# Middle-sized experts of a MoE kernel as half and quarter blocks, with a new order of the ranks

## The chip, the cores and the metric

The kernel runs on one core of a Trainium2 chip. A time is device microseconds of one execution. Three runs of the kernel before are given, and their median stands for it. Beside them there is one profiled execution, whose trace is read here.

## The reference

One decoder block on 512 tokens of width 1024, all float32: a mixer (Mamba-2 SSD branch, pooling branch, gates), then a mixture of 32 experts, four to a token, then a norm. The change touches the experts alone:

```python
logits = xt @ w_router + b_router
top_val, top_idx = lax.top_k(logits, 4);  gate = softmax(top_val)
def expert_block(xblk, e):                  # rows of tokens of one expert
    gu = xblk @ w_gu[e] + b_gu[e]           # 1024 -> 2048
    glu, lin = split(gu, 2);  glu = min(glu, 7);  lin = clip(lin, -7, 7)
    act = glu * sigmoid(1.702 * glu) * (lin + 1)
    return act @ w_down[e] + b_down[e]      # 1024 -> 1024
y = segment_sum(yb * row_gate, row_tok)
```

How many of the 512 tokens go to an expert differs from expert to expert and is known only at run time.

## The kernel before, in words

After the mixer and the router the kernel sorts the 32 experts by their number of tokens into ranks. A table `ROOM` gives each rank its room, in rows of tokens: rank 0 has 128, ranks 1 to 15 have 64, ranks 16 to 26 have 72 to 96 (eleven ranks), ranks 27 to 30 have 108 to 128, rank 31 has 192. What does not fit is done in a loop behind everything, which runs as often as there are overflowing blocks. Each rank is a **step** of the main loop, and `order_of_ranks` writes the sequence of steps out by hand. In it `s` is a rank with room for 64, `f` one of ranks 16 to 30, `None` rank 31. Before, it reads: rank 0, s s, five pairs f s, rank 31, s, five pairs f s, five f in a row, s s.

Every step needs the expert's whole weights, 12 MB: eight 1 MB pieces of `w_gu` (128 rows of the contraction by 2048) and four of `w_down` (two contraction chunks by 1024). SyncE's queue fetches them (L772) into a ring of eleven 1 MB buffers, in the order of use; a fetch waits until its buffer has been read.

Step `u` does `up(u)`, the products with `w_gu`, and then `down(u-1)`, the products with `w_down` of the step before; hooks between the pieces hold the small work: `prep(u+2)` (which tokens, and a gather of their rows by GpSimd), `turned(u+1)` (transposes of the gathered rows), `act_turn` (activation of step u and its transposes), `send` (scaling by the gate and a scatter-add into DRAM by GpSimd). PSUM has two pools of four banks, `mm` and `ss`.

A rank is computed in one of two forms:

- **whole** (room over 64): `esplit` splits each piece into a rounded part (ScalarE, L117) and a remainder (VectorE, L118), and each product is three TensorE matmuls of 128 columns by 512 in the rounded type (L1119, L1120, L1121): 96 in `up`, 48 in `down`.
- **half** (room up to 64): no split; the 1 MB piece is used as it is, in float32, with 64 tokens as the stationary operand (L1114). Two output chunks lie on the two halves of the 128 PSUM partitions (`rows_of`), so that two matmuls of 64 columns use the array side by side: 32 in `up`, 16 in `down`. The trace has two records for each of these float32 matmuls.

Bias products (L1108 whole, L1105 half) open each group of banks, so their rows in the trace mark where an `up` (bank `mm`) or a `down` (bank `ss`) begins.

Of the kernel before, what the change touches and what calls it, by code (L numbers as in the profile page):

```python
# [20 lines left out]
P = 128  # L21
# [38 lines left out]


def order_of_ranks():
    s, f = iter(range(FIXED, FIXED + SMALL)), iter(range(FIXED + SMALL, NE - 1))
    kinds = [s, s] + [f, s] * 5 + [None, s] + [f, s] * 5 + [f] * 5 + [s, s]
    return list(range(FIXED)) + [next(k) if k else NE - 1 for k in kinds]


# [1 line left out]
def hybrid_block(ctx: ExitStack, tc: tile.TileContext, cst, cols, rows, xt, xf, wad0, wada, bada,  # L69
# [902 lines left out]
    def overflow_table():  # L972
        cap = cs[:, C_CAP:C_CAP + NE]
        ex, dcap, deid = rk["tmp"][:, 0:NE], rk["tmp"][:, NE:2 * NE], rk["eid"]
        nbk, tmp = T_("nbk", NE), T_("tmpe", NE)
        tt(ex, rk["cnt"], cap, ALU.subtract)
        V.tensor_scalar(nbk, ex, 0.0, None, op0=ALU.is_gt)
        for lim in (128.0, 256.0, 384.0):
            V.tensor_scalar(tmp, ex, lim, None, op0=ALU.is_gt)
            tt(nbk, nbk, tmp, ALU.add)  # L980
        ce = T_("ce", NE)
        V.tensor_tensor_scan(ce, ones[:, 0:NE], nbk, 0.0, op0=ALU.mult, op1=ALU.add)
        V.memset(dcap, 0.0)
        tt(dcap[:, 0:NE - 1], cap[:, 1:NE], cap[:, 0:NE - 1], ALU.subtract)
        stt(dcap, nbk, -128.0, dcap, ALU.mult, ALU.add)
        tt(tmp[:, 0:NE - 1], deid[:, 1:NE], deid[:, 0:NE - 1], ALU.subtract)
        V.memset(tmp[:, NE - 1:NE], 0.0)
        ruf, euf, ubase, eui, novi = T_("ruf", OVER), T_("euf", OVER), T_("ubase", OVER), T_("eui", OVER, I32), T_("novi", 1, I32)
        V.tensor_copy(novi, ce[:, NE - 1:NE])
        for u in range(0, OVER, 16):  # L990
            us_ = slice(u, u + 16)
            lev, lwv = (T_(t, 512).rearrange("p (u e) -> p u e", u=16) for t in ("q16", "q15"))
            tt(lev, ce.unsqueeze(1).to_broadcast([P, 16, NE]), iota[:, us_].unsqueeze(2).to_broadcast([P, 16, NE]), ALU.is_le)
            V.tensor_reduce(ruf[:, us_], lev, axis=AX.X, op=ALU.add)
            tt(lwv, lev, dcap.unsqueeze(1).to_broadcast([P, 16, NE]), ALU.mult)
            V.tensor_reduce(ubase[:, us_], lwv, axis=AX.X, op=ALU.add)
            tt(lwv, lev, tmp.unsqueeze(1).to_broadcast([P, 16, NE]), ALU.mult)
            V.tensor_reduce(euf[:, us_], lwv, axis=AX.X, op=ALU.add)
        V.tensor_scalar(ruf, ruf, float(NE - 1), None, op0=ALU.min)
        stt(ubase, iota[:, 0:OVER], 128.0, ubase, ALU.mult, ALU.add)  # L1000
        V.tensor_scalar(ubase, ubase, float(room(0)), None, op0=ALU.add)
        V.tensor_copy(eui, euf)
        return ruf, euf, ubase, eui, novi
# [4 lines left out]

    turned_rot = Rot(["q11"])

    class Op:
        def __init__(self, t, half):
            self.t, self.half = t, half
            if half:
                self.c = [t[:, k % 4 * P + k // 4 * 64:k % 4 * P + k // 4 * 64 + 64] for k in range(KD)]
            else:
                self.h, self.l = ([t[:, r * 1024 + k * P:r * 1024 + (k + 1) * P] for k in range(KD)] for r in range(2))

# [4 lines left out]

    def slots(i, pos, n_, xe):
        half = n_ <= 64
        s4 = T_(("a2", "wrt")[i % 2 if i != "x" else 0], 4 * P, BF16)
        for b in range(NB):
            o = s4[:, b * P:(b + 1) * P]  # L1030
            if half:
                V.tensor_scalar(o.rearrange("p (h m) -> p h m", h=2), iota1[:, 0:64].unsqueeze(1).to_broadcast([P, 2, 64]),
                                pos(b), None, op0=ALU.is_equal)
            else:
                V.tensor_scalar(o, iota1, pos(b), None, op0=ALU.is_equal)
        ps = bank("ss")
        for b in range(NB):
            sb_ = s4[:, b * P:(b + 1) * P]
            TE.matmul(ps[:, 0:2], sb_, tokc[:, 0:2], start=b == 0, stop=False)
            TE.matmul(ps[:, 0:2], sb_, tokc[:, 2 + 2 * b:4 + 2 * b], start=False, stop=b == NB - 1)  # L1040
        n = i if i == "x" else i % 6
        st = dict(s4=s4, ps=ps, xe=xe, n=n, half=half, rows=P if half else min(n_, P))
        ix_ = T_(f"ixs_{n}", 2)
        stt(ix_[:, 0:1], ps[:, 1:2], cs[:, C_NP:C_NP + 1], cs[:, C_P5:C_P5 + 1], ALU.mult, ALU.add)
        tt(ix_[:, 0:1], ps[:, 0:1], ix_[:, 0:1], ALU.add)
        if half:
            stt(ix_[:, 1:2], ix_[:, 0:1], 2.0, cs[:, C_H:C_H + 1], ALU.mult, ALU.add)
        idx = T_(f"idx_{n}", 1, I32)
        V.tensor_copy(idx, ix_[:, 1:2] if half else ix_[:, 0:1])
        src, lim, xe = (h_d2, 2 * T - 1, xe[:, 0:512]) if half else (h_d, T - 1, xe)  # L1050
        if i != 0:
            n_ = st["rows"]
            G.indirect_dma_start(xe[0:n_, :], None, src, bass.IndirectOffsetOnAxis(ap=idx[0:n_, :], axis=0), bounds_check=lim, oob_is_err=False)
        st.update(idx=idx, ixf=ix_[:, 0:1])
        return st
# [35 lines left out]
        return ps[n // 2][n % 2 * 64:n % 2 * 64 + 64, :]  # L1091

    lastp = []

# [2 lines left out]
            bias_rows(x, ps, sel, n0)  # L1099

    def bias_rows(x, ps, sel, n0):
        for n, p in enumerate(ps):
            if x.half:
                c = n0 // 2 + n
                TE.matmul(p, sel["wide"], bt[:, c * 512:(c + 1) * 512], start=True, stop=False)  # L1105
            else:
                h, c = (n0 + n) % 2, (n0 + n) // 2
                TE.matmul(p, sel["cols"][:, h:h + 1].to_broadcast([P, P]), bt[:, c * 512:(c + 1) * 512], start=True, stop=False)  # L1108

    def products(x, ps, k, hl, o, n0=0):  # L1110
        stop = k == KD - 1
        if x.half:
            for i in range(2):
                lastp[:] = [TE.matmul(rows_of(ps, n0 + i), x.c[k], hl[:, o + i * 512:o + (i + 1) * 512], start=False, stop=stop).ins]  # L1114
            return
        hi, lo = hl
        for i in range(2):
            p, h, l = ps[n0 + i], hi[i], lo[i]
            TE.matmul(p, x.h[k], h, start=False, stop=False)  # L1119
            TE.matmul(p, x.h[k], l, start=False, stop=False)  # L1120
            lastp[:] = [TE.matmul(p, x.l[k], h, start=False, stop=stop).ins]  # L1121
# [3 lines left out]
            yield o, esplit(r[:, o:o + 1024]) if full else None  # L1125

    def up(xs, sel, w, hooks):
        pss = [[bank("ss" if i else "mm") for _ in range(2 if x.half else 4)] for i, x in enumerate(xs)]
        for x, ps in zip(xs, pss):
            biases(x, ps, sel, 0)  # L1130
        for k in range(KD):
            r = eload(w, "wu", k)
            for o, hl in ahead.pop(0) if ahead else pieces(r, not xs[0].half):
                for x, ps in zip(xs, pss):
                    products(x, ps, k, r if x.half else hl, o, o // 512)
            for f in hooks.get(k, ()):
                f()
        return pss
# [14 lines left out]
    def act_rows(pg, pl_):  # L1153
# [5 lines left out]
        stt(l, l, 1.0, t, ALU.add, ALU.mult)  # L1159
        return l  # L1160

    def act_turn(l, aT, n):
        pt = turn_tile(l)
        if aT.half:
# [10 lines left out]
    def send(ps, st, tag="y"):  # L1175
        half, y = st["half"], T_(tag, 512 if st["half"] else 1024)
        for n, p in enumerate(ps):
            yn = y[:, n * 512:(n + 1) * 512]
            S.activation(yn, p, AF.Copy, scale=st["gate"])  # L1179
            G.tensor_tensor(yn, yn, gaf2[0] if half else gaf[n], op=ALU.mult)  # L1180
        dst, lim = (y_d2, 2 * (T + P) - 1) if half else (y_d, T + P - 1)
# [94 lines left out]
    def select(u):  # L1276
# [5 lines left out]
        for h in range(2 if both else 0):  # L1282
            hs = slice(h * 64, (h + 1) * 64)
            G.tensor_copy(wides[u % 2][hs, hs], e[hs, :].to_broadcast([64, 64]))

    def prep(u):
        if u < NE:
            sts[u] = slots(u, pos_of(u), room(order[u]), xe2[u % 2])
            if u > FIXED:
                slot_gates(sts[u], gv_of(u))  # L1290

    def turned(u):
        if u < NE:
            xs_[u] = [turn(sts[u], Rot(["y"]) if u == 1 else x_rot)]


# [62 lines left out]
    for u in range(NE + 1):  # L1359
        hooks = {}  # L1360
        if u < NE:
            w, sel = weights_of(u), sel_of(u)
            pre = {k: list(f) for k, f in extra.get(u, {}).items()}
            if u != 0:
                pre.setdefault(0, []).append(lambda: prep(u + 2))
            if u == big - 2:
                pre.setdefault(4, []).append(prep_x)
            if pend:
# [3 lines left out]
                pre[n] = [f] + pre.get(n, [])  # L1372
            begin = []
            pss = up(xs_[u], sel, w, pre)
            aTs = [op_of(Rot(["q16"]) if u == 1 else a_rot, xs_[u][0].half)]
            hooks = {n: [f] for n, f in enumerate(acts(pss[0], aTs[0]))}
            if u == big:
                aTs.append(op_of(Rot(["b12"]), True))
                lx = act_rows(*pss[1])
# [12 lines left out]
        else:  # L1392
# [6 lines left out]
            else:  # L1399
                send(psd[0], sts[v])  # L1400
                if len(psd) > 1:
                    pend.append(lambda p=psd[1]: send(p, sts["x"], "q16"))
        if u < NE:
            prev = (u, aTs)

# [136 lines left out]
```

## Time and profile before

| | |
|---|---|
| runs | 1824.81, 1825.79, 1829.6 us; median 1825.79 us |
| profiled execution | 1824.71 us, of which the span of instructions is 1822.9 us |
| TensorE busy in the span | 1739.8 us (95%) |
| VectorE, ScalarE, GpSimd busy | 1211.0, 947.8, 238.7 us |
| HBM traffic | 527.81 MB, 290 GB/s over the span |
| granted TensorE clock, mean | 0.995 of full speed |
| experts | from the first bias product at 696.87 us to the end |

The 1.8 us between span and time lie around the span. A busy TensorE in this profile is one that has a matmul in flight, which is not yet one that works at its peak.

### The profile page before, as it was taken

The numbers are of one execution on the slowest core, as the hardware profiler recorded it, in microseconds if no ns is written. First come the engines' busy times: TensorE is split into PE (matmuls) and PEld (weight loads), VectorE is DVE, ScalarE is ACT, GpSimd is POOL, SyncE is SP. The second block draws the span as 40 slices with busy tenths as digits, with TensorE's granted clock in tenths as the row PEclk, the third lists the DMA queues.
The fourth block names the chain that finished last, engine by engine and source line by source line (L and its number), as shares of the span: only waits on it lengthen the run. The fifth ranks groups of instructions, "written<-read, shape, count | busy, mean of one in ns | idle before, by whom it ended". The sixth has DMA issues, their size and how long they took to land. (4 is left out here: it accounts for less than half of the span.)

```text
span 1822.9 us, 23331 instructions
## 1 busy us (share of the span) xinstructions
PE 1739.8 (95%) x8353; PEld 1160.5 (64%) x8353; DVE 1211.0 (66%) x1803; ACT 947.8 (52%) x1458; POOL 238.7 (13%) x215
## 2 busy tenths in 40 slices
PE   6999999999999999999999999999999999999995
PEld 3787787877778777456556455464565565677741
DVE  5888686857574548666567556375585586799933
ACT  4533455637372346356455455265465465677833
POOL 0000001010100002121121211122112112222111
PEclk9999999999999999999999999999999999999998
DMA  9265333353553457999999999889999999998894
GB/s 358 75 243 220 116 119 135 116 118 114 127 151 135 170 220 296 360 410 401 408 407 403 400 392 335 307 324 378 399 404 396 402 405 364 412 348 340 311 375 189
DMA packets 86344, 527.81 MB, mean 290 GB/s; under 512 B 11737, under 2 KB 12377, under 8 KB 27600
## 3 DMA queue, kind: packets, MB, share of 16 engines
q1 hardware_dynamic: 74160, 498.14, 69.9%
q0 software_dynamic: 11184, 25.50, 6.6%
q10 hardware_dynamic: 880, 2.64, 0.4%
q8 instruction: 67, 1.10, 0.2%
q14 instruction: 53, 0.43, 0.1%
HBM read 502.89 MB, written 25.77 MB: 290 GB/s over the span
## 5 line engine op out<-in xcount | busy, mean ns | idle before, releaser
L118 DVE TENSOR_TENSOR wl<-r,wh 128x1024 fp32r<-128x1024 f32 x246 | 301.8, 1251 | 106.4 <-ACT wh L117 105.4
L117 ACT ACTIVATE wh<-r 128x1024 fp32r<-128x1024 f32 x246 | 254.6, 1058 | 125.1 <-PE mm L266 48.4
L118 DVE TENSOR_TENSOR wl<-S,wh 128x1024 fp32r<-128x1024 f32 x186 | 229.3, 1268 | 32.9 <-ACT wh L117 32.4
L1120 PE MATMUL mm<-wl,S 128*128 128x512 f32 x540 | 214.2, 397 | 8.1 <-DVE wl L118 7.9
L117 ACT ACTIVATE wh<-S 128x1024 fp32r<-128x1024 f32 x186 | 190.2, 1057 | 54.2 <-PE mm L1121 30.2
L1121 PE MATMUL mm<-wh,S 128*128 128x512 f32 x540 | 212.9, 394 | 0.0
L265 PE MATMUL mm<-S,wh 128*128 128x512 f32 x512 | 204.9, 401 | 3.9 <-ACT S L117 3.9
L267 PE MATMUL mm<-S,wl 128*128 128x512 f32 x512 | 203.8, 398 | 1.5 <-DVE wl L118 1.5
L266 PE MATMUL mm<-S,wh 128*128 128x512 f32 x512 | 204.1, 399 | 0.0
L1119 PE MATMUL mm<-wh,S 128*128 128x512 f32 x540 | 182.1, 400 | 1.9 <-ACT wh L117 1.4
L1155 DVE TENSOR_SCALAR q<-mm 128x512 f32<-128x512 f32 x49 | 33.5, 688 | 151.7 <-PE mm L1114 124.4
L1156 ACT ACTIVATE q<-q 128x512 f32<-128x512 f32 x50 | 31.6, 634 | 191.7 <-DVE q L1155 191.6
L1119 PEld LDWEIGHTS mm<-wh,S 128*128 128x128 f32 x540 | 101.1, 188 | 39.4 <-issue 9.7
L1120 PEld LDWEIGHTS mm<-wl,S 128*128 128x128 f32 x540 | 101.3, 188 | 37.2 <-DVE wl L118 14.2
L265 PEld LDWEIGHTS mm<-S,wh 128*128 128x128 f32 x512 | 96.3, 188 | 30.6 <-ACT S L117 4.1
L1121 PEld LDWEIGHTS mm<-wh,S 128*128 128x128 f32 x540 | 101.4, 188 | 21.8
L266 PEld LDWEIGHTS mm<-S,wh 128*128 128x128 f32 x512 | 96.3, 188 | 26.2 <-issue 4.6
L267 PEld LDWEIGHTS mm<-S,wl 128*128 128x128 f32 x512 | 96.3, 188 | 25.9 <-issue 2.2
L1120 PE MATMUL ss<-wl,S 128*128 128x512 f32 x240 | 98.8, 412 | 3.1 <-DVE wl L118 3.1
L1121 PE MATMUL ss<-wh,S 128*128 128x512 f32 x240 | 94.8, 395 | 0.0
L1114 PE MATMUL mm<-S,S 128*64 128x512 f32 x408 | 94.6, 595 | 0.0
L1180 POOL TENSOR_TENSOR y<-y,q 128x512 f32<-128x512 f32 x47 | 63.5, 1363 | 209.0 <-ACT y L1179 208.9
(500 smaller groups left out, 3072.8 us busy)
## 6 DMA issues: line engine op xcount, KB each, us to landing
S<-in_wgu SPq DMA_DIRECT2D x113, 1024.0 KB, 10.9
r<-in_wgu SPq DMA_DIRECT2D x97, 1024.0 KB, 9.9
S<-in_wdn SPq DMA_DIRECT2D x61, 1024.0 KB, 12.3
r<-in_wdn SPq DMA_DIRECT2D x44, 1024.0 KB, 13.9
bc<-in_wgu SPq DMA_DIRECT2D x23, 1024.0 KB, 11.5
Z<-in_wgu SPq DMA_DIRECT2D x23, 1024.0 KB, 9.5
r<-in_wada SPq DMA_DIRECT2D x16, 1024.0 KB, 6.0
r<-in_wx SPq DMA_DIRECT2D x12, 1024.0 KB, 6.4
```

Source lines behind the costliest of these rows:

```text
L117: S.activation(hi, src, AF.Copy)
L118: V.tensor_tensor(lo, src, hi.bitcast(F32), op=ALU.subtract)
L265: TE.matmul(ps, a, hh(k), start=k == 0, stop=False)
L266: TE.matmul(ps, a, hl(k), start=False, stop=False)
L267: TE.matmul(ps, b, hh(k), start=False, stop=k == KD - 1)
L1114: lastp[:] = [TE.matmul(rows_of(ps, n0 + i), x.c[k], hl[:, o + i * 512:o + (i + 1) * 512], start=False, stop=stop).ins]
L1119: TE.matmul(p, x.h[k], h, start=False, stop=False)
L1120: TE.matmul(p, x.h[k], l, start=False, stop=False)
L1121: lastp[:] = [TE.matmul(p, x.l[k], h, start=False, stop=stop).ins]
L1155: V.tensor_scalar(g, pg, LIM, None, op0=ALU.min)
L1156: S.activation(t, g, AF.Tanh, scale=ALPHA / 2)
L1180: G.tensor_tensor(yn, yn, gaf2[0] if half else gaf[n], op=ALU.mult)
```

## The change

The eleven ranks with room for 72 to 96 get a third form, **half and quarter**: the first 64 tokens go as a half block, the other 8 to 32 as a quarter block, in which the stationary operand is 32 columns wide and four output chunks lie on the four quarters of the PSUM partitions (`rows32`), so that four matmuls of 32 columns may stand side by side. Nothing is split for such a rank. It has its own slots, gather, transposes, activation (`act_quarter`), gate scaling and scatter (under the tag `q16`, one step later). In `down` the quarter block takes two contraction chunks at once, two quarters each, and `send` adds the two partial sums. The order is now: rank 0, s s, twice (w s f f f s), s, rank 31, s s, w s f f f, s w s f f s s s, where `f` is one of the eleven and `w` one of the four larger ranks, which stay whole. The table of overflow borrows another buffer.

```diff
 def order_of_ranks():
-    s, f = iter(range(FIXED, FIXED + SMALL)), iter(range(FIXED + SMALL, NE - 1))
-    kinds = [s, s] + [f, s] * 5 + [None, s] + [f, s] * 5 + [f] * 5 + [s, s]
+    s, f, w = (iter(r) for r in (range(FIXED, FIXED + SMALL), range(FIXED + SMALL, NE - 5), range(NE - 5, NE - 1)))
+    kinds = [s, s] + ([w, s] + [f] * 3 + [s]) * 2 + [s, None, s, s] + [w, s] + [f] * 3 + [s, w, s, f, f, s, s, s]
...
     def slots(i, pos, n_, xe, quarter=0):
...
+        if quarter:
+            G.memset(s4.rearrange("p (h m) -> p h m", m=64)[:, :, quarter:64], 0.0)
...
+    def rows32(ps, n):
+        o = n % 2 * 64 + n // 2 * 32
+        return ps[0][o:o + 32, :]
...
     def bias_rows(x, ps, sel, n0):
+        if x.quarter:
+            for n in range(4 if x.quarter == "up" else 2):
+                c, h = (n0 + n) // 2, n % 2
+                TE.matmul(rows32(ps, n), sel["wide"][:, h * 64:h * 64 + 32].bitcast(F32), bt[:, c * 512:(c + 1) * 512].bitcast(F32),
+                          start=True, stop=False)
+            return
...
     def products(x, ps, k, hl, o, n0=0):
         stop = k == KD - 1
+        if x.quarter == "up":
+            for n in range(4 if n0 else 0):
+                lastp[:] = [TE.matmul(rows32(ps, n), x.c[k], hl[:, n * 512:(n + 1) * 512], start=False, stop=stop).ins]
+            return
+        if x.quarter:
+            for n in range(4 if k % 2 else 0):
+                kk = k - 1 + n // 2
+                lastp[:] = [TE.matmul(rows32(ps, n), x.c[kk], hl[:, n * 512:(n + 1) * 512], start=kk == 1, stop=kk >= KD - 2).ins]
+            return
...
+    def act_quarter(p):
+        g, t, l = g_rot(), t_rot(), l_rot()
+        V.tensor_scalar(g, p, LIM, None, op0=ALU.min)
+        S.activation(t, g, AF.Tanh, scale=ALPHA / 2)
+        V.tensor_scalar(l, p, LIM, -LIM, op0=ALU.min, op1=ALU.max)
+        for o in (0, 64):
+            V.tensor_scalar(l[o:o + 32, :], p[o + 32:o + 64, :], LIM, -LIM, op0=ALU.min, op1=ALU.max)
+        stt(t, t, 1.0, g, ALU.add, ALU.mult)
+        stt(l, l, 1.0, t, ALU.add, ALU.mult)
+        return l
...
     def send(ps, st, tag="y"):
...
+            if st["quarter"]:
+                S.activation(yn, p, AF.Copy)
+                for o in (0, 64):
+                    S.activation(yn[o:o + 32, :], p[o + 32:o + 64, :], AF.Copy)
+                tt(yn, yn, p, ALU.add)
+                p = yn
             S.activation(yn, p, AF.Copy, scale=st["gate"])
...
+    def mid(u):
+        return u < NE and 64 < room(order[u]) <= 96
...
+    def prep_quarter(u):
+        pu = T_("pu", 4)
+        V.tensor_scalar(pu, rk["pos"][:, :, order[u]], 64.0, None, op0=ALU.subtract)
+        sts[u, 1] = slots(u, lambda b: pu[:, b:b + 1], 64, xe2[u % 2][:, 512:D], room(order[u]) - 64)
+        slot_gates(sts[u, 1], gv_of(u))
...
             pss = up(xs_[u], sel, w, pre)
-            aTs = [op_of(Rot(["q16"]) if u == 1 else a_rot, xs_[u][0].half)]
+            aTs = two_ops(a_rot, "down") if mid(u) else [op_of(Rot(["q16"]) if u == 1 else a_rot, xs_[u][0].half)]
             hooks = {n: [f] for n, f in enumerate(acts(pss[0], aTs[0]))}
+            if mid(u):
+                hooks[1] = [lambda: act_turn(act_quarter(pss[1][0]), aTs[1], 0)]
```

**Place 1: TensorE, the start of an `up` of a rank with room for 72 to 96.** Names are those of the program without buffer numbers: `wh` and `wl` are the two parts of a split piece, `S` and `bc` behind the arrow buffers of the weight ring or the turned tokens. Before, as a whole block:

```order
L1108 MATMUL mm_7410<-bt_383,sel_694_5147 128x512
L1108 MATMUL mm_7411<-bt_383,sel_694_5147 128x512
L1119 MATMUL mm_7410<-wh_713_5237,S_1013_7350 128x512
L1119 MATMUL mm_7411<-wh_713_5237,S_1013_7350 128x512
L1120 MATMUL mm_7410<-wl_715_5239,S_1013_7350 128x512
L1121 MATMUL mm_7410<-wh_713_5237,S_1013_7350 128x512
```

The same place in the change:

```order
L1123 MATMUL mm_7992<-bt_383,sw_696_5149 128x512
L1123 MATMUL mm_7993<-bt_383,sw_696_5149 128x512
L1117 MATMUL mm_7994<-bt_383,sw_696_5149 32x512 x4
L1142 MATMUL mm_7992<-bc_1121_8001,S_1113_7930 64x512 x2
L1142 MATMUL mm_7993<-bc_1121_8001,S_1113_7930 64x512 x2
L1133 MATMUL mm_7994<-bc_1121_8001,S_1113_7930 32x512 x4
L1142 MATMUL mm_7992<-S_1127_8040,S_1113_7930 64x512 x2
L1142 MATMUL mm_7993<-S_1127_8040,S_1113_7930 64x512 x2
L1133 MATMUL mm_7994<-S_1127_8040,S_1113_7930 32x512 x4
```

Twelve matmuls a piece have become eight, and the width of the stationary operand goes from 64 columns to 32 and back at each of the eight pieces.

**Place 2: TensorE, the start of a `down` of such a rank.** `r`, `Z` and `bc` are buffers of the weight ring or the turned activations, `q` the activations. Before, as a whole block:

```order
L1108 MATMUL ss_7277<-bt_383,sel_694_5147 128x512
L1108 MATMUL ss_7278<-bt_383,sel_694_5147 128x512
L1067 MATMUL ss_7307<-cst_70,q_1009_7301 128x128 x3
L1119 MATMUL ss_7277<-wh_713_5237,S_971_7106 128x512
L1119 MATMUL ss_7278<-wh_713_5237,S_971_7106 128x512
```

And in the change, with another such rank behind it:

```order
L1123 MATMUL ss_8363<-bt_383,sw_696_5149 128x512
L1117 MATMUL ss_8364<-bt_383,sw_696_5149 32x512 x2
L1142 MATMUL ss_8363<-r_1177_8368,S_1140_8142 64x512 x4
L1138 MATMUL ss_8364<-r_1177_8368,S_1140_8142 32x512 x4
L1074 MATMUL ss_8386<-cst_70,q_1180_8380 128x128 x4
L1142 MATMUL ss_8363<-Z_8395,S_1140_8142 64x512 x4
L1138 MATMUL ss_8364<-Z_8395,S_1140_8142 32x512 x4
L1074 MATMUL ss_8415<-cst_70,q_1185_8407 128x128 x4
```

The transposes of the activations (`cst` is the identity) stood ahead of nearly all products; now a whole piece stands ahead of the first four, and another ahead of the second four. A change of width stands at every line but one.

## Rows read from the trace of the kernel before

**Rows 1.** The page's 40 equal slices of the span: busy tenths.

```profile
PE   6999999999999999999999999999999999999995
...
DMA  9265333353553457999999999889999999998894
```

**Rows 2.** Busy time per engine in two stretches; behind the engines PEclk, DMA share, GB/s.

```profile
1420.00:1460.00 40.00, 37.95 (x190) 18.72 (x189) 19.33 (x32) 16.59 (x31) 5.06 (x6) 1.00 1.01 410
...
1660.00:1700.00 40.00, 37.90 (x179) 29.75 (x178) 37.56 (x42) 31.74 (x41) 8.72 (x6) 1.00 0.89 329
```

**Rows 3.** TensorE in order of time, f and s by turns: start, duration, line, tiles.

```profile
964.42 0.72 PE L1108 MATMUL ss<-bt,sel 128*128 128x512 f32 x2
...
979.04 1.09 PE L1108 MATMUL mm<-bt,sel 128*128 128x512 f32 x4
...
1003.53 0.39 PE L1105 MATMUL ss<-bt,sw 128*128 128x512 f32 x1
...
1015.10 0.73 PE L1105 MATMUL mm<-bt,sw 128*128 128x512 f32 x2
...
1030.52 0.73 PE L1108 MATMUL ss<-bt,sel 128*128 128x512 f32 x2
1032.80 0.52 PE L1067 MATMUL ss<-cst,q 128*128 128x128 f32 x3 [1.55 <-DVE q L111]
```

**Rows 4.** The same view, one f of the five in a row.

```profile
1615.41 1.09 PE L1108 MATMUL mm<-bt,sel 128*128 128x512 f32 x4
...
1639.36 0.63 PE L1108 MATMUL ss<-bt,sel 128*128 128x512 f32 x2
...
1655.47 1.10 PE L1108 MATMUL mm<-bt,sel 128*128 128x512 f32 x4
```

**Rows 5.** The same view, the next to last half block's `down`.

```profile
1779.30 0.50 PE L1105 MATMUL ss<-bt,sw 128*128 128x512 f32 x1
...
1787.48 0.50 PE L1105 MATMUL ss<-bt,sw 128*128 128x512 f32 x1
```

**Rows 6.** Waits from 800 to 1780 us, SyncE's queue, then the engines: total, times, longest.

```profile
SPq L772 <- DVE wl L118: 387.1, 159, 6.2
SPq L772 <- PE ss L1114: 164.8, 49, 5.0
SPq L772 <- PE mm L1114: 131.7, 98, 4.4
...
PEld mm L1114 <- DMA S<-in_wdn: 1.6, 7, 0.3
```

**Rows 7.** TensorE in order of time: products of half blocks, 64 columns wide.

```profile
944.24 1.94 PE L1114 MATMUL ss<-S,r 128*64 128x512 f32 x8
946.11 0.18 PE L1039 MATMUL ss<-tokc,a 128*128 128x2 bf16 x1
...
954.02 1.89 PE L1114 MATMUL mm<-Z,S 128*64 128x512 f32 x8
955.74 1.89 PE L1114 MATMUL mm<-bc,S 128*64 128x512 f32 x8
```

**Rows 8.** The same view, matmuls 32 columns wide, in the mixer.

```profile
43.09 1.92 PE L244 MATMUL ss<-S,cact 128*32 128x512 f32 x16
44.94 0.50 PE L265 MATMUL mm<-S,wh 128*128 128x512 f32 x1
...
141.03 1.06 PE L204 MATMUL mm<-b,E 64*32 64x512 f32 x8
142.02 1.06 PE L401 MATMUL mm<-q,ones 128*32 128x512 f32 x6
143.01 0.50 PE L265 MATMUL mm<-S,wh 128*128 128x512 f32 x1
```

**Rows 9.** Groups by line from 700 us on: busy us, mean ns, idle before.

```profile
L118 DVE TENSOR_TENSOR wl<-S,wh 128x1024 fp32r<-128x1024 f32 x185 | 228.1, 1268 | 32.3 <-ACT wh L117 31.8
...
L1183 POOL DMA_INDIRECT y_d<-y,idx x30 | 66.6, 2220 | 8.9 <-POOL y L1180 8.6 <-issue 0.3
...
L1075 ACT ACTIVATE S<-mm,colf 128x64 f32<-128x64 f32 x112 | 34.8, 421 | 15.6 <-PE mm L1067 15.6
```

More of the change, by code (lines that the diff above doesn't have):

```diff
@@ L974, in overflow_table @@
         ex, dcap, deid = rk["tmp"][:, 0:NE], rk["tmp"][:, NE:2 * NE], rk["eid"]
-        nbk, tmp = T_("nbk", NE), T_("tmpe", NE)
+        nbk, tmp = T_("mx", NE), T_("tmpe", NE)
         tt(ex, rk["cnt"], cap, ALU.subtract)
@@ L1011, in hybrid_block, with __init__ @@
     class Op:
-        def __init__(self, t, half):
-            self.t, self.half = t, half
+        def __init__(self, t, half, quarter=None):
+            self.t, self.half, self.quarter = t, half, quarter
             if half:
-                self.c = [t[:, k % 4 * P + k // 4 * 64:k % 4 * P + k // 4 * 64 + 64] for k in range(KD)]
+                w = 32 if quarter else 64
+                self.c = [t[:, k % 4 * P + k // 4 * 64:k % 4 * P + k // 4 * 64 + w] for k in range(KD)]
             else:
@@ L1022, in hybrid_block, with slots @@
     h_d2, y_d2 = (d.rearrange("t (h n) -> (t h) n", h=2) for d in (h_d, y_d))
-    def slots(i, pos, n_, xe):
+    def slots(i, pos, n_, xe, quarter=0):
         half = n_ <= 64
         s4 = T_(("a2", "wrt")[i % 2 if i != "x" else 0], 4 * P, BF16)
+        if quarter:
+            G.memset(s4.rearrange("p (h m) -> p h m", m=64)[:, :, quarter:64], 0.0)
         for b in range(NB):
@@ L1031, in slots @@
             if half:
-                V.tensor_scalar(o.rearrange("p (h m) -> p h m", h=2), iota1[:, 0:64].unsqueeze(1).to_broadcast([P, 2, 64]),
+                m = quarter or 64
+                V.tensor_scalar(o.rearrange("p (h m) -> p h m", h=2)[:, :, 0:m], iota1[:, 0:m].unsqueeze(1).to_broadcast([P, 2, m]),
                                 pos(b), None, op0=ALU.is_equal)
@@ L1040, in slots @@
             TE.matmul(ps[:, 0:2], sb_, tokc[:, 2 + 2 * b:4 + 2 * b], start=False, stop=b == NB - 1)
-        n = i if i == "x" else i % 6
-        st = dict(s4=s4, ps=ps, xe=xe, n=n, half=half, rows=P if half else min(n_, P))
+        n = i if i == "x" else f"c{i % 4}" if quarter else i % 6
+        st = dict(s4=s4, ps=ps, xe=xe, n=n, half=half, quarter=quarter,
+                  rows=64 + quarter if quarter else P if half else min(n_, P))
         ix_ = T_(f"ixs_{n}", 2)
@@ L1127, in up @@
     def up(xs, sel, w, hooks):
-        pss = [[bank("ss" if i else "mm") for _ in range(2 if x.half else 4)] for i, x in enumerate(xs)]
+        pss = [[bank("ss" if i and not x.quarter else "mm") for _ in range(1 if x.quarter else 2 if x.half else 4)] for i, x in enumerate(xs)]
         for x, ps in zip(xs, pss):
@@ L1284, in select, with two_ops @@
             G.tensor_copy(wides[u % 2][hs, hs], e[hs, :].to_broadcast([64, 64]))
+    def mid(u):
+        return u < NE and 64 < room(order[u]) <= 96
     def prep(u):
         if u < NE:
-            sts[u] = slots(u, pos_of(u), room(order[u]), xe2[u % 2])
+            sts[u] = slots(u, pos_of(u), 64 if mid(u) else room(order[u]), xe2[u % 2])
             if u > FIXED:
                 slot_gates(sts[u], gv_of(u))
-    def turned(u):
-        if u < NE:
+    def prep_quarter(u):
[3 more added lines that the diff above has]
+        slot_gates(sts[u, 1], gv_of(u))
+    def two_ops(rot, way):
+        t = rot(1024)
+        return [Op(t[:, 0:512], True), Op(t[:, 512:1024], True, way)]
+    def turned(u):
+        if mid(u):
+            xs_[u] = two_ops(x_rot, "up")
+            for x, st in zip(xs_[u], (sts[u], sts[u, 1])):
+                norm_cols(x.t, turn_tile(st["xe"], "mm"), 0, 64)
+        elif u < NE:
             xs_[u] = [turn(sts[u], Rot(["y"]) if u == 1 else x_rot)]
@@ L1365, in hybrid_block @@
                 pre.setdefault(0, []).append(lambda: prep(u + 2))
+            if mid(u + 2):
+                pre.setdefault(2, []).append(lambda: prep_quarter(u + 2))
             if u == big - 2:
@@ L1374, in hybrid_block @@
             pss = up(xs_[u], sel, w, pre)
-            aTs = [op_of(Rot(["q16"]) if u == 1 else a_rot, xs_[u][0].half)]
+            aTs = two_ops(a_rot, "down") if mid(u) else [op_of(Rot(["q16"]) if u == 1 else a_rot, xs_[u][0].half)]
             hooks = {n: [f] for n, f in enumerate(acts(pss[0], aTs[0]))}
+            if mid(u):
+                hooks[1] = [lambda: act_turn(act_quarter(pss[1][0]), aTs[1], 0)]
             if u == big:
@@ L1401, in hybrid_block @@
                 if len(psd) > 1:
-                    pend.append(lambda p=psd[1]: send(p, sts["x"], "q16"))
+                    pend.append(lambda p=psd[1], st=sts["x" if v == big else (v, 1)]: send(p, st, "q16"))
         if u < NE:
```

## The prediction

> **What bounds the kernel now.** I read the page's slices first, then the busy time of two stretches, then TensorE's rows in order of time, and the waits last. The slices show TensorE at 9 tenths in all but the first and the last, and the DMA engines as full only from the middle on, where the experts run [rows 1]. So the question is which of the two sets the pace there. Where f and s alternate, TensorE is busy 38 of 40 us and the DMA share is 1.01 at 410 GB/s; in the row of five f TensorE is just as busy, VectorE is at 37.6, and the DMA share falls to 0.89 at 329 GB/s [rows 2]. The granted clock is 1.00 in both, which is the level of 2.4 GHz. The waits decide: SyncE's queue waits 683 us in three lines alone for buffers that the engines have not yet read, while the largest of TensorE's waits for a piece of weights in that window sums to 1.6 us [rows 6]. The weights come early enough; TensorE sets the pace. I therefore cost the change in TensorE's own order.
>
> The bias rows cut that order into blocks. Between halves, a whole block takes 24.49 us in `up` (979.04 to 1003.53) and 14.62 in `down` (964.42 to 979.04), 39.1 together; a half takes 15.42 in `up` and 11.57 in `down`, 27.0 [rows 3]. In the row of five a whole takes 40.06 [rows 4]. A half's `down` without a whole beside it takes 8.18 [rows 5]. One `down` of a whole starts with TensorE standing 1.55 us for the activation on VectorE [rows 3].
>
> **What the new form costs.** Four half products of a piece take 1.72 us (954.02 to 955.74, eight records) [rows 7], 0.43 each. For 32 columns, sixteen records, that is eight products, take 1.85 us to the next wider matmul, and eight records of another group 0.99 [rows 8]. So four of them side by side cost 0.86, and 0.13 is left over in each case. That rest is the price of changing the tile: it is 0.13 from 64 rows by 32 columns to 128 by 32 (141.03 to 142.02), 0.13 back to full width (142.02 to 143.01, where three products cost what four do) [rows 8], and 0.15 from 64 columns to 128 (944.24 to 946.11, less 1.72) [rows 7]. No row shows 64 columns to 32 and back; I take 0.13, the row nearest to it, since it too goes between two narrow tiles. The bounds are 0, if these two widths could follow each other freely, and 0.15.
>
> The Trainium skill, TensorEngine Tiling, Key Properties, says that changing the tiling mode drains TensorE, while going from tile to tile within a mode does not. The 0.13 to 0.15 of rows 7 and 8 agree with it, and by that rule the switch between 64 and 32 columns has to cost as much, which speaks against this change.
>
> By the new order of TensorE a piece is four half products, a change, four quarter products, a change: 1.72 + 0.86 + 0.26 = 2.84 us. `up` has eight pieces, 22.7. A half's `up` has 15.42 - 8 x 1.72 = 1.66 for bias, transposes of the next block and their changes; that stays, and the quarter's bias adds 0.86 + 0.26, its slot products some 0.3 (estimate, from the 64-column run that they interrupt): 25.8. `down` has four pieces, 11.4; the rest of a half's lean `down` is 8.18 - 4 x 1.72 = 1.30; the quarter's bias 1.12 and four more transposes 0.6 (three take 0.52 in rows 3): 14.4. Together **40.2 us**. I add 0.4 for waits. They should be small: by the order of the change a whole piece, 2.84 us, now stands ahead of each four transposes, and in rows 3 it was the lack of such cover that cost 1.55. So an f costs 40.6, against 39.1 or 40.06 as a whole block. That 144 products become 96 saves nothing on TensorE: those that remain are float32 products with two records each.
>
> **The sum.** Before: ten f between halves and five in a row, 10 x 39.1 + 5 x 40.06 = 591.3. After: four w between halves, which keep 39.1, and eleven f, 4 x 39.1 + 11 x 40.6 = 603.0. That is +11.7. The four halves that stand ahead of a group of f no longer share VectorE with a split: their `down` goes from 11.57 to about 10.3 (8.18, four transposes 0.6, slot products 0.5, up to 1.0 of waiting for the second activation): -5.1. The halves behind the groups get two sets of slot products into their `up`, each of which leaves a product without a partner beside it; at 0.3 a set, an estimate from the 0.43 of a lone product, +2.4. Sum +9.0. The rest of the order moves blocks that keep their prices.
>
> At nothing I put: the splits that vanish, 24 of 1268 ns for each f on VectorE [rows 9], some 335 us of busy time in all, since only their waits count and those are within the measured 39.1 and 40.06; the 11 more scatters of 2.2 us and as many gathers on GpSimd [rows 9], which is busy 5 to 9 us of 40 [rows 2]; the quarter's activation, six VectorE operations more per f on an engine that loses 30 us per f; and the fetches on SyncE, whose number and order by step stay. Their cover is the two steps between `prep` and use; gone, each would cost a gather's landing per step. The weights have room: a group w s f f f s eats 72 pieces in some 215 us (39.1 + 2 x 27 + 3 x 40.6), 3.0 us a piece, where f and s by turns eat one in 66.1 / 24 = 2.75.
>
> Against the profiled execution, 1824.7 us, this gives **1834 us**; the median shown is 1.1 us higher. The unknowns of this case: waits of 0 instead of 0.4 give -4 us, and slot sets that cost nothing another -6, so 1824; a wait of 1.55 in each f [rows 3] and changes of 0.15 (28 in an f, counted below) give +19, 1853.
>
> **The rivals.**
>
> *The two widths follow each other without a drain.* An f has 2 x 8 + 2 x 4 changes between products and 4 around its biases, 28 in all; eleven f have 308, at 0.13 that is 40 us. Then an f costs 37.0, less than a whole, and the time is 1834 - 40 = **1794 us**, faster. It decides from 0.10 us per change down: at 0.10 the sum is even. For it speaks that no row shows just this pair; against it, that each change of tile that does have a row costs 0.13 or more [rows 7, 8].
>
> *Halves in a row run out of weights.* Three halves end the sequence now, two before. From the first `up` on they and the last f eat 40 pieces in about 84 us. At 410 GB/s [rows 2] a piece comes every 2.56 us, 33 in that time, so 7 must lie ready at its start. The ring has eleven buffers and the f ahead are slow eaters, so mostly they do. With only 5 ready, two or three pieces come late: +6, **1840 us**.
>
> *New waits in each f.* Its `up` holds three `mm` banks of four, so the transposes of half and quarter of the next f share one bank: the second four wait until ScalarE has read the first, eight operations of 421 ns [rows 9], 3.4 us, under one piece of 2.84. If ScalarE is late there as well, behind the quarter's four scaling passes, it becomes 2 to 3 us per f: 11 x 2.4 = +26, **1860 us**. Against it stands ScalarE's load, which loses 24 splits per f.
>
> *The change does not do what it says:* quarter products do not stand four side by side but one after another, 0.43 each. Then each of the 12 groups costs 0.86 more: 11 x 10.3 = +113, **1947 us**. The 32-column rows speak against it [rows 8].
>
> **How the numbers follow.** About 0.3% (5.5 us) is what a measurement of this kernel can tell from no change. The forecast has 0.53; of that 0.03 falls below 1819, 0.14 within 5.5 us of now, 0.36 above, as its own range is 1824 to 1853. No drain gets 0.24, nearly all of it faster, since one missing row carries 40 us. Late weights get 0.08, new waits 0.13, both slower but for 0.01, and quarters in file 0.02. Sum: faster 0.26, same 0.16, slower 0.58. The range goes from 1790, which takes in some two thirds of the case without drain, to 1856, which takes in the forecast and the lesser part of the waits; outside are about 0.2.
>
> **What would show it.** Right: in a row of three f the bias rows lie 40 to 41 us apart; eight records of 64 columns, eight of 32, and the next 64 come at steps near 1.85 and 0.99; the f no longer show VectorE's split among TensorE's waits; SyncE still waits for buffers most of the time. Wrong: steps of 1.72 and 0.86 (no drain) or of 1.72 for the quarter too (no concurrency), transposes (L1074) waiting for ScalarE for over 1 us in each f, or half products waiting for DMA in the last 80 us. The forecast fails altogether if blocks that I left alone, halves or w, change their length by over 1 us each.

## The result, and the profile after

The changed kernel took a median of 1859.33 us (1857.34 to 1862.32, four runs), the kernel before 1827.69 us (1824.81 to 1831.27, four runs): a ratio of 1.0179, with a 95% interval of 1.0163 to 1.0195. It is slower by about 32 us. The forecast had the sign, but at 1834 us only a quarter of the amount, and the result lies 3 us above the upper end of the range. The profiled execution took 1858.18 us, of which the span is 1856.3 us, 33.4 us more than before.

I cut TensorE's order at the bias rows again, as in [rows 3, 4]. Sums over the steps of a kind, in us:

| kind of step | before | change, as forecast | change, measured |
|---|---|---|---|
| eleven f (mid rooms) and four w, before all whole | 592.3 | 603.0 | 439.3 + 181.7 = 621.0 |
| one f, mean | 39.1 to 40.06 | 40.6 | 39.94 |
| the four w | as f | 39.1 each | 39.2, **51.4**, 39.9, **51.2** |
| rank 31 | 66.8 | unchanged | 69.3 |
| halves, less the last `down` | 391.4 | 388.7 | 393.1 |

So 28.7 of the 33 us came in f and w together, and 24 of those in two blocks of a kind that I had left alone. TensorE in order of time, one f of the changed kernel (start, duration, line, tiles), answers to [rows 3, 4] and to [rows 7, 8]:

```profile
882.27 0.74 PE L1123 MATMUL mm<-bt,sw 128*128 128x512 f32 x2
882.94 1.06 PE L1117 MATMUL mm<-bt,sw 128*32 128x512 f32 x8
...
884.52 1.94 PE L1142 MATMUL mm<-S,S 128*64 128x512 f32 x8
886.39 1.06 PE L1133 MATMUL mm<-S,S 128*32 128x512 f32 x8
...
890.84 1.94 PE L1142 MATMUL mm<-r,S 128*64 128x512 f32 x8
892.70 1.07 PE L1133 MATMUL mm<-r,S 128*32 128x512 f32 x8
893.70 1.94 PE L1142 MATMUL mm<-r,S 128*64 128x512 f32 x8
...
908.02 0.51 PE L1123 MATMUL ss<-bt,sw 128*128 128x512 f32 x1
...
922.06 0.73 PE L1123 MATMUL mm<-bt,sw 128*128 128x512 f32 x2
```

`up` is 25.75 us (forecast 25.8), `down` 14.04 (forecast 14.4). Four half products step 1.86 to 1.87 us, four quarter products 1.00: beyond 1.72 and 0.86 that is 0.14 to 0.15 for each change of width. So a change of width is not free in either direction, and the quarters do stand side by side. SyncE's queue still waits for buffers (waits from 800 to 1815 us: total, times, longest), as in [rows 6]:

```profile
SPq L772 <- PE mm L1133: 223.1, 85, 5.8
SPq L772 <- PE ss L1142: 154.1, 55, 6.8
SPq L772 <- PE mm L1142: 114.4, 88, 3.2
SPq L772 <- PE ss L1138: 112.8, 38, 3.7
```

That is 604 us in four lines. Weights are not what is missing. The stretches that answer to [rows 2], one in a row of three f and one with a long w (busy time per engine; then PEclk, DMA share, GB/s), show where it is:

```profile
882.00:922.00 40.00, 40.00 (x225) 10.17 (x223) 6.45 (x10) 8.80 (x22) 3.36 (x4) 1.00 0.93 347
...
992.00:1032.00 40.00, 31.71 (x131) 21.54 (x128) 25.32 (x32) 20.48 (x23) 9.18 (x7) 0.87 0.83 316
```

In the f TensorE has no hole, and VectorE has little to do. In the w TensorE is short of 8 us, at a mean granted clock of 0.87. Here is its order there:

```profile
992.87 1.19 PE L1126 MATMUL mm<-bt,sel 128*128 128x512 f32 x4
...
1005.57 1.10 PE L1147 MATMUL mm<-wh,S 128*128 128x512 f32 x4
1013.62 0.80 PE L1148 MATMUL mm<-wl,S 128*128 128x512 f32 x1 [6.96 <-DVE wl L118]
...
1019.34 0.48 PE L1149 MATMUL mm<-wh,S 128*128 128x512 f32 x1
...
1029.36 0.39 PE L1123 MATMUL ss<-bt,sw 128*128 128x512 f32 x1
```

This `up` takes 36.5 us instead of 24.5. TensorE stands 6.96 us for the remainder `wl` of a split, which VectorE makes. VectorE's rows, and then GpSimd's, say why it is late:

```profile
1001.10 3.39 DVE L118 TENSOR_TENSOR wl<-bc,wh 128x1024 fp32r<-128x1024 f32 x2
1012.26 0.15 DVE L1056 CAST idx_c<-ixs_c 128x1 int32<-128x1 f32 x1 [7.78 <-DMA y_d<-q,idx_c]
1012.34 2.36 DVE L118 TENSOR_TENSOR wl<-S,wh 128x1024 fp32r<-128x1024 f32 x2
```

```profile
994.37 1.61 POOL L1228 DMA_INDIRECT y_d<-y,idx  x1 [0.28 <-POOL y L1225]
...
1004.53 1.47 POOL L1228 DMA_INDIRECT y_d<-q,idx_c  x1 [2.26 <-DMA y_d<-y,idx]
1012.69 1.79 POOL L1060 DMA_INDIRECT S<-h_d,idx_c  x1 [6.70 <-DVE idx_c L1056]
```

The cast writes the row numbers of the quarter block two steps ahead (`prep_quarter(u+2)`) into the buffer `idx_c`, of which there are four (`f"c{i % 4}"`, line 1047). The quarter block of step u-2 has the same name, and its scatter was issued only now, in `up(u)`, at 1004.53. The scatter reads the buffer until it has landed, 7.7 us later. VectorE works in order, so the next split stands behind the cast. In the new order u-2 and u+2 are both f at two steps, 9 and 25 (rank 0 is step 0), and both are w. The list of VectorE's waits over the whole execution has just these two:

```profile
DVE idx_c L1056 <- DMA y_d<-q,idx_c: 15.9, 2, 8.1
```

The clock adds to it. The same windows, cut finer:

```profile
1005.00:1010.00 5.00, 1.67 (x8) 1.01 (x6) 0.00 (x0) 1.76 (x2) 0.99 (x1) 0.93 1.01 403
1010.00:1015.00 5.00, 1.38 (x3) 1.16 (x4) 2.74 (x4) 0.00 (x0) 1.79 (x1) 0.50 0.14 38
1015.00:1020.00 5.00, 5.00 (x14) 3.88 (x13) 4.34 (x4) 2.12 (x2) 0.00 (x0) 0.55 0.83 306
1020.00:1025.00 5.00, 5.00 (x24) 4.06 (x23) 3.19 (x3) 3.93 (x4) 0.00 (x0) 1.00 0.94 342
```

After TensorE has stood, the granted clock is 0.50, the level of 1.2 GHz. From 1013.62 to 1019.34 thirteen products take 5.72 us, 0.44 each, where at full clock they take 0.23: 2.7 us more. With the 7.0 us of standing that makes 9.7 of the 12.0. The other 2.3 were lost before it, at the start of the `up`; the first experiment, without the stop, keeps 2.4.

### The profile page after: what moved, and what is told of

It reads as the page before. It is cut to its first block, busy times and chain, and to the rows that moved or that the text cites. A ratio compares the mean times of both kernels' runs of the same rounds, so it can differ in the third digit from the quotient of the medians.

```text
span 1856.3 us, 24309 instructions
## 1 busy us (share of the span) xinstructions
PE 1776.2 (96%) x9112; PEld 955.7 (51%) x9112; DVE 911.6 (49%) x1649; ACT 713.9 (38%) x1293; POOL 257.1 (14%) x270
## 5 line engine op out<-in xcount | busy, mean ns | idle before, releaser
L118 DVE TENSOR_TENSOR wl<-r,wh 128x1024 fp32r<-128x1024 f32 x150 | 181.1, 1224 | 89.6 <-ACT wh L117 81.0
L117 ACT ACTIVATE wh<-r 128x1024 fp32r<-128x1024 f32 x150 | 155.5, 1056 | 110.7 <-PE mm L266 48.5
L1142 PE MATMUL mm<-S,S 128*64 128x512 f32 x696 | 165.8, 600 | 0.1
L1142 PE MATMUL mm<-r,S 128*64 128x512 f32 x608 | 147.1, 600 | 0.0
L1082 ACT ACTIVATE S<-mm,colf 128x64 f32<-128x64 f32 x288 | 89.4, 423 | 138.9 <-PE mm L1074 138.7
L267 PEld LDWEIGHTS mm<-S,wl 128*128 128x128 f32 x512 | 96.3, 188 | 25.9 <-issue 2.2
L1142 PEld LDWEIGHTS mm<-S,S 128*64 128x64 f32 x696 | 45.4, 136 | 94.3 <-issue 78.8
L1148 PE MATMUL mm<-wl,S 128*128 128x512 f32 x188 | 78.0, 415 | 14.9 <-DVE wl L118 14.7
L118 DVE TENSOR_TENSOR wl<-S,wh 128x1024 fp32r<-128x1024 f32 x66 | 79.4, 1238 | 13.3 <-ACT wh L117 13.3
L117 ACT ACTIVATE wh<-S 128x1024 fp32r<-128x1024 f32 x66 | 66.9, 1053 | 34.9 <-PE mm L1149 19.1
L1149 PE MATMUL mm<-wh,S 128*128 128x512 f32 x188 | 76.2, 405 | 0.0
```

The source lines that it names most:

```text
L117: S.activation(hi, src, AF.Copy)
L118: V.tensor_tensor(lo, src, hi.bitcast(F32), op=ALU.subtract)
L267: TE.matmul(ps, b, hh(k), start=False, stop=k == KD - 1)
L1082: S.activation(out_[:, o], pt[:, o], AF.Identity, scale=colf[:, 8 + f:9 + f], bias=colf[:, f:f + 1])
```

## The experiments

Times are medians; ratios stand against the kernel before on the same chip, with their 95% intervals.

### Three index names instead of four

```diff
-        n = i if i == "x" else f"c{i % 4}" if quarter else i % 6
+        n = i if i == "x" else f"c{i % 3}" if quarter else i % 6
```

> The change with one edit: the quarter blocks' index, slot and gate buffers rotate over three names instead of four. Theory A: in the changed kernel VectorE stops for 7.8 us, twice, because the index of the quarter of step u+2 goes into the buffer that the scatter of the quarter of step u-2 still reads (four steps apart, four names); with three names no two quarters in flight share one. Expected: 1835 us (1831 to 1839), the two long ups of a whole block (36.5 us) back at 24.5 to 25, and no granted clock of 0.5 at that place. Theory B: the splits of a whole block start late because the steps before it split nothing (buffers, order of ScalarE's work), whatever the names: 1857 to 1862, and the stop stays. Three names could also cost if each quarter now waits for the one three steps before: over 1862.

Measured: 1843.31 us (1843.0 to 1843.57), 1.0102 [1.0084, 1.0119]. One character takes 16 us off, 8 less than expected. VectorE has no wait for a scatter any more. Both long w fall by 9.6 us each, to 41.8 and 41.6 us, but not to 39.1. TensorE in `up` of the same w, and the granted clock there:

```profile
995.83 1.19 PE L1126 MATMUL mm<-bt,sel 128*128 128x512 f32 x4
...
998.23 0.73 PE L1147 MATMUL mm<-wh,S 128*128 128x512 f32 x2 [0.28 <-ACT wh L117]
999.18 0.74 PE L1147 MATMUL mm<-wh,S 128*128 128x512 f32 x2 [0.22 <-ACT wh L117]
...
1022.75 0.39 PE L1123 MATMUL ss<-bt,sw 128*128 128x512 f32 x1
```

```profile
996.00:1000.00 4.00, 3.00 (x21) 1.74 (x22) 2.54 (x9) 3.91 (x6) 3.42 (x3) 1.00 1.02 419
1000.00:1004.00 4.00, 4.00 (x11) 3.07 (x11) 4.00 (x6) 4.00 (x5) 3.30 (x2) 0.57 1.03 383
```

This `up` is 26.9 us. ScalarE is full at its start (3.91 of 4 us): the passes of `send` for the f behind are mixed with the first splits. TensorE stands in pieces, some 1 us in all, and then runs 4 us at a granted clock of 0.57. So theory A holds for the stop itself, and something like theory B, late splits after steps that split nothing, is left over. No run changes the order of ScalarE's passes alone; but where the quarter products are gathered (below), the first two splits stand ahead of most of those passes, and the same two w take 39.3 and 39.1 us. Of the 24 us that I had expected from it, the two w keep 5, and the halves are 1.5 us longer in sum than in the changed kernel. Rank 31 (69.3) and the f are as they were there. The part ahead of the experts, which the edit leaves alone, happened to take 3.0 us more in this profile.

### The form alone, and the order alone

The first kernel keeps the half and quarter blocks and three names, and has the order of before; the second has the new order and computes all fifteen ranks whole (`mid` returns False).

```diff
-    s, f, w = (iter(r) for r in (range(FIXED, FIXED + SMALL), range(FIXED + SMALL, NE - 5), range(NE - 5, NE - 1)))
-    kinds = [s, s] + ([w, s] + [f] * 3 + [s]) * 2 + [s, None, s, s] + [w, s] + [f] * 3 + [s, w, s, f, f, s, s, s]
+    s, f = iter(range(FIXED, FIXED + SMALL)), iter(range(FIXED + SMALL, NE - 1))
+    kinds = [s, s] + [f, s] * 5 + [None, s] + [f, s] * 5 + [f] * 5 + [s, s]
```

> As e1_idx3, but with the order of ranks of the kernel before (f and s by turns, five in a row at the end, of which four are whole). By the block costs an f is 40.2 wherever it stands, so the order matters little: 1836 us (1832 to 1842). If the three in a row of the new order are worth something (weights stream ahead over the slow steps) this is slower than e1 by over 5 us; if the row costs (three waits in a row), faster by over 5.

```diff
-        return u < NE and 64 < room(order[u]) <= 96
+        return False
```

> The new order alone: no rank is computed as half and quarter, all sixteen above 64 stay whole. By the block costs of before (39.1 between halves, 40.1 in a row) seven f more stand in a row, five fewer at the end: +2, and three halves at the end 0 to +5: 1830 us (1826 to 1836). If the order is what costs, 1845 or more.

Measured: the form alone 1832.89 us, 1.0046 [1.003, 1.0062]; the order alone 1836.02 us, 1.0067 [1.0047, 1.0087]. Against the 1825.02 of before these are +7.9 and +11.0, 18.9 together, and with three names both at once cost 18.3. So the times nearly add up, and the fourth name adds 16 more. Block by block they do not: alone, the order costs 9.9 us in f and w; on top of the form it costs 11.8 us in the halves, of which fewer then stand between two f. The form behaves as forecast: eleven f of 40.0 us, 8.2 us more in sum, and the halves shorter by 8.6. What is left of its price lies mostly in rank 31, which takes 71.7 us instead of 66.8. The order costs more than I thought also where all blocks are whole, since three of these in a row take 40.8, 42.5 and 38.6 us instead of 39.1 each. The row of five in the kernel before begins in the same way, with 40.7 and 42.4 us; I had taken its third block, 40.06, for all five. TensorE's waits from 880 to 905 us in the kernel with the order alone, at the start of the second of three:

```profile
PE mm L1147 <- ACT wh L117: 1.4, 2, 1.2
```

```profile
885.00:890.00 5.00, 3.04 (x13) 1.66 (x13) 4.31 (x8) 4.97 (x6) 3.93 (x3) 0.92 1.01 415
890.00:895.00 5.00, 5.00 (x18) 3.93 (x17) 4.78 (x5) 2.22 (x4) 0.00 (x0) 0.74 1.03 375
```

ScalarE is full again (4.97 of 5 us) and its splits late, and the granted clock falls behind the hole. That this is all of the order's price was not tried.

### The fourth name in the order of before

Here a stop on VectorE should meet steps that are f themselves. The diff is that of the order above, on the change as it was.

> e3_oldorder with the four names of the changed kernel. In the old order the f stand two steps apart, so two quarters four steps apart share a name at seven steps, and each time VectorE should stop for about 8 us at the cast of the index. But each of these steps is itself an f, whose products need no split. Theory A, the stop costs only where TensorE needs VectorE at once: as e3, 1833 us (1830 to 1838), with the stops in the trace. Rival, any such stop holds TensorE (slots, activation): seven times 7 to 12 us, 1880 or more.

Measured: 1832.09 us, 1.004 [1.0027, 1.0053], the same as with three names. Yet VectorE stops at seven places, for 84.6 us in all:

```profile
DVE idx_c L1056 <- DMA y_d<-q,idx_c: 84.6, 7, 14.3
```

The stop is five times as long in sum and costs nothing. TensorE's rows have no idle time during any of the seven: behind the cast stand the gate and selection matrices, and no split. Only together with the new order, which puts a w between two f, does it cost 16 us.

### Fewer changes of width

The quarter products of four pieces (in `down` of two) are gathered into one run, in the new order and in the old one, with three names. Of the edit only the part in `up` is shown; it does the same in `down`, and holds the half products of a piece in their order.

```diff
...
-            for n in range(4 if n0 else 0):
-                lastp[:] = [TE.matmul(rows32(ps, n), x.c[k], hl[:, n * 512:(n + 1) * 512], start=False, stop=stop).ins]
+            with tc.issue_after(lastp[0]):
+                for i, r in enumerate(hl if n0 and k % 4 == 3 else ()):
+                    kk = k - 3 + i
+                    for n in range(4):
+                        lastp[:] = [TE.matmul(rows32(ps, n), x.c[kk], r[:, n * 512:(n + 1) * 512], start=False, stop=kk == KD - 1).ins]
...
```

> As e1_idx3, and the quarter products of four pieces of up (two of down) are gathered behind the half products of the same pieces; TensorE's order then has 127 changes of tile width fewer (459 instead of 586 in the experts), with the same products. Theory A, each change drains and costs 0.14 us: 127 x 0.14 = 18 us less than e1, 1817 us (1813 to 1823). Theory B, the 0.13 to 0.15 at each change is only the end of a group of products, which grouping moves but does not save: as e1, 1835. Theory C, pieces held longer make the weights late: SyncE's fetches wait more, half products wait for DMA, 1840 or more.

> e3_oldorder (old order, three names) with the quarter products gathered over four pieces as in e2_group42. In e2 an f cost 38.7 us instead of 39.9; if that comes from the changes of width it holds in any order: 11 x 1.2 = 13 us below e3, 1820 us (1815 to 1826), faster than the kernel before. If in the old order the halves beside an f lose what the f gains (pieces held longer, halves waiting for weights), 1830 or more.

Measured: new order 1830.78 us, 1.0028 [1.0013, 1.0042], 12.5 less than with three names alone; old order 1825.19 us, 1.0001 [0.9988, 1.0014], 7.7 less and just level with the kernel before; this one still has a long `up` of 33.5 us in one f, which the next section explains. TensorE's order has 459 changes of width instead of 586 in the new order. At 0.14 those 127 are worth 18 us, and 12.5 came, which lies between theories A and B and is a balance: an f takes 38.74 instead of 39.94, 13.2 us in eleven, and the w give 5.0 more, but the halves lose 7.0 and rank 31 another 2.2. TensorE at the start of one:

```profile
884.45 1.94 PE L1147 MATMUL mm<-S,S 128*64 128x512 f32 x8
887.09 0.65 PE L1074 MATMUL mm<-cst,S 128*128 128x128 f32 x4 [0.69 <-ACT S L1082]
887.67 5.37 PE L1147 MATMUL mm<-r,S 128*64 128x512 f32 x24
892.97 1.06 PE L1136 MATMUL mm<-S,S 128*32 128x512 f32 x8
893.85 2.76 PE L1136 MATMUL mm<-r,S 128*32 128x512 f32 x24
```

Three pieces now run 5.30 us without a change, but the second four transposes wait 0.69 us for ScalarE to read the bank of the first. That is the wait that I gave 2 to 3 us per f among the rivals. With quarter products between the transposes it was covered; without them it is there in seven of the eleven f, at about a quarter of that size.

### Each w beside halves, and a second stop

Now an order that keeps every w and most f between halves, five names for each kind of block, and the gathered products:

```diff
-    kinds = [s, s] + [f, s] * 5 + [None, s] + [f, s] * 5 + [f] * 5 + [s, s]
+    kinds = [s, s] + [w, s] + [f, s] * 3 + [w, s] + [None, s] + [w, s] + [f, s] * 3 + [w, s] + [f] * 5 + [s, s]
...
-        n = i if i == "x" else f"c{i % 3}" if quarter else i % 6
+        n = i if i == "x" else f"c{i % 5}" if quarter else i % 5
```

> A version from the block times: quarter products gathered as in e2, five names for half and for quarter blocks, and an order that has one w or f between halves throughout, w next to rank 31 and at the start, and five f in a row at the end (0 s s, w s, three f s, w s, rank 31 s, w s, three f s, w s, five f, s s). Against e5: five f in a row at 38.7 instead of one f and four w at 40.3, -8; rank 31 and the first steps keep the times of the kernel before, -8 to -10; three w at 39.1 among the halves for f at 38.4, +2. 1806 us (1800 to 1818). If a row of five f holds weights or gathers back, 1820 or more.

Measured: 1830.67 us, 1.0022 [1.0011, 1.0032], a miss by 25 us. Two `up` are long again, a w of 33.5 us and an f of 35.6, and this time not for an index. TensorE's waits from 1200 to 1225 us, GpSimd's rows, and the bias rows of that w:

```profile
PE ss L1045 <- POOL wrt L1033: 5.0, 1, 5.0
```

```profile
1205.11 2.31 POOL L1238 DMA_INDIRECT y_d<-y,idx  x1 [0.28 <-POOL y L1235]
1206.92 1.82 POOL L1235 TENSOR_TENSOR q<-q,q 128x512 f32<-128x512 f32 x1
1217.66 1.58 POOL L1238 DMA_INDIRECT y_d<-q,idx_x  x1 [8.93 <-DMA y_d<-y,idx]
1218.69 0.98 POOL L1033 MEMSET wrt<- 128x384 bf16 x1
```

```profile
1203.00 1.20 PE L1126 MATMUL mm<-bt,sel 128*128 128x512 f32 x4
...
1236.46 0.39 PE L1123 MATMUL ss<-bt,sw 128*128 128x512 f32 x1
```

A scatter-add waits until the one before it into the same array has landed: here that of rank 31's second block is ready at 1208.7 and waits 8.93 us. GpSimd stands for that long, and behind it stands the fill of the next quarter's selection matrices (L1033), which TensorE needs for the slot products. So I moved that one fill to VectorE, in three kernels:

```diff
-            G.memset(s4.rearrange("p (h m) -> p h m", m=64)[:, :, quarter:64], 0.0)
+            V.memset(s4.rearrange("p (h m) -> p h m", m=64)[:, :, quarter:64], 0.0)
```

> As e7_mixed_group (1830.67), with the one fill of the quarter's selection matrices (L1033, 0.3 to 1.0 us, seven to eleven times) on VectorE instead of POOL. In e7 POOL stood 8.9 and 6.7 us before the quarter's scatter, until the half's scatter had landed, with this fill behind it, and TensorE stood 5.0 and 6.3 us for the fill and then ran at a granted clock of 0.50; the two ups were 33.5 and 35.6 us long instead of 24.5 and 25. Theory (POOL behind the landing of the scatter): TensorE no longer waits for the fill, both ups come back, 1830.7 - 9.0 - 10.6 = 1811 us, 1807 to 1817. Rival (the gather that is issued behind the same scatter is what the step really needs): the stop moves to the transposes of the gathered rows, 1826 to 1831.

> As e5_old_group (1825.19, one up of 33.5 us behind a POOL wait of 5.0 us, TensorE standing 4.7 us for the fill), with the same move of the fill to VectorE. Theory: 1825.2 - 8.5 = 1817 us, 1813 to 1820, faster than the kernel before by about 0.5%. Rival (as for e8): 1823 to 1826.

> As e2_group42 (1830.78; the changed order of steps, three names, grouped products), with the same move of the fill. There TensorE has no wait for the fill in its list of waits, so both theories say no change, 1829 to 1832; a gain of over 3 us would say that the fill on POOL costs elsewhere too.

Measured, against 1825.85 us for the kernel before: 1812.66 us, 0.9926 [0.9913, 0.9939], with the mixed order; 1818.77 us, 0.996 [0.9947, 0.9973], with the old one; 1831.1 us, 1.0028 [1.0018, 1.0038], in the change's order, where TensorE had no such wait. All three are as the theory of the stopped queue had it. The mixed order, its w again, on TensorE and then on GpSimd:

```profile
1203.18 1.20 PE L1126 MATMUL mm<-bt,sel 128*128 128x512 f32 x4
...
1229.08 0.39 PE L1123 MATMUL ss<-bt,sw 128*128 128x512 f32 x1
```

```profile
1217.47 1.65 POOL L1238 DMA_INDIRECT y_d<-q,idx_x  x1 [8.55 <-DMA y_d<-y,idx]
1219.42 2.06 POOL L1060 DMA_INDIRECT S<-h_d,idx  x1 [0.30 <-DVE wl L118]
```

GpSimd waits about as long as before, 8.55 us, and the gather behind it is as late (1219.42, and 1219.84 with the fill on GpSimd), but `up` takes 25.9 us instead of 33.5. So it was the fill, and not the gather, that TensorE missed. This version, with the mixed order, five names, the gathered products and the moved fill, is faster than both kernels, by 0.74% than the one before.

## Why the prediction was wrong, point by point

- **TensorE sets the pace, not the weights:** right. SyncE's queue waits for buffers throughout, and none of the long blocks waits for a piece.
- **What an f costs:** right within 0.7 us: 39.94 against 40.6. A change of width costs 0.14 to 0.15, where I took 0.13 from two other pairs of widths; the case without a drain is out, and so are quarters one after another. The waits that I added, 0.4 in each f, are not there: TensorE has no idle time in any f, so the covers that I named held. The rival of quarters in file was priced too low, since 0.43 is what a product costs with a partner beside it; alone it costs twice that, as the rows of rank 31 below show.
- **The halves:** those ahead of a group have a `down` of 10.12 us (10.3 forecast), two of those behind one an `up` of 16.07 (16.0), one of 15.63. Not foreseen were the `up` behind the second group, 18.68 us, of which TensorE waits 1.9 for selection matrices from VectorE, and halves ahead of a w, with a `down` of 12.4 to 12.5 instead of 11.57. The sum is +1.7 instead of -2.7.
- **"Four w between halves, which keep 39.1":** this step of the sum failed, and it alone made 24 of the 33 us. Two took 51.4 and 51.2. I priced a w by blocks in which VectorE had splits and little else to do, but by the new order the preparation of an f two steps ahead and the scatter of one two steps behind are done within a w. I had even counted these 11 scatters and gathers "at nothing" by GpSimd's busy time, which is indeed small (9.2 of 40 us with the long w in it); but a scatter's price lies in what it holds after its issue, an index buffer for 7.7 us, and in who wants that buffer. The sentence on their cover spoke of gathers alone.
- **"The rest of the order moves blocks that keep their prices":** rank 31 took 2.5 us more. The order alone, with whole blocks, cost 11 us, a price that my sum did not have, as it compared blocks by their kind and not by what the block ahead leaves to do; that this is ScalarE's work is read from the traces and was not tried by itself.
- **The forecast for the list of waits** was that f no longer show VectorE's split. They don't; the w do, with 14.7 us in four waits on L1148 from 800 us on, and of that 14.3 in the two stops.
- **The rival of new waits in each f (1860 us)** gives nearly the measured time, but by a mechanism that is not there: an f is shorter than forecast, and the waits are in two w. The forecast did name as its failure that blocks left alone, halves or w, change by over 1 us each.

With the measured values the sum closes: 621.0 - 592.3 = 28.7 for f and w, 1.7 for halves, 2.5 for rank 31, -0.5 for rank 0; ahead of the experts 1.2 us less, from the last `down` on 2.2 more. Together these are the 33.4 us of the span.

The 2.5 us of rank 31 are neither a wait nor the clock: TensorE is busy all through it, at a granted clock of 1.00. In its `up`, four products of its half block have lost the partner that ran beside them, and the two records of a lone product take as long as the four of a pair. Before, and in the change:

```profile
1114.98 1.08 PE L1114 MATMUL ss<-r,b 128*64 128x512 f32 x4
```

```profile
1252.55 1.07 PE L1142 MATMUL ss<-S,b 128*64 128x512 f32 x2
```

That is 2.0 us in `up`. The order alone, with whole blocks, has the same lone products and the same 69.3 us.

Open are what separates these pairs, and how much of the price of the order alone is the clock and how much ScalarE's lateness.

## What to carry to other kernels

Where a change adds a block that is prepared and sent off in its neighbours' time, list for each buffer name that is used by turns (here `c0` to `c3`) who reads it last and when that read ends, and look at what stands behind the waiting instruction on its engine in the step where it happens. The same stop cost nothing seven times in steps that needed nothing from that engine, and some 10 us each in two that did. A block's price holds only beside the neighbours with which it was measured.

## What was not expected of the hardware

- A scatter of a quarter block, issued at 1004.53, let go of its index buffer 7.7 us later, and a scatter-add into the same array waited up to 8.93 us for the one before, with GpSimd's queue standing.
- A hole of 7 us on TensorE was followed by work at a granted clock of 0.50 to 0.55, here until 1019 us, where each product takes 0.44 instead of 0.23 us. With three names, some 1 us of standing in pieces was also followed by 0.57 over 4 us; as much standing at the same place in the changed kernel was followed by 1.00. So a wait can cost more than it lasts: 2.7 us on top of 7.0 here.
- Going between stationary tiles of 64 and 32 columns cost 0.14 to 0.15 us each way. The Trainium skill, TensorEngine Tiling, Key Properties, has the drain; its size is from these rows.
